# A transformer trunk layer on one core: the first modulation piece cut in two with the context tokens brought in later, more late-modulation chunks ahead of the gates, pooled products two chunks later, and the scores' maximum taken negated

## The chip, the core and the metric

The kernel runs on one core of a Trainium2 chip. The metric is the time of one execution on the device in microseconds (us). The engines are named as in the profile: PE (TensorE: matrix products, with its weight loads as PEld), DVE (VectorE), ACT (ScalarE), POOL (GpSimd) and SP (SyncE, which here issues nearly all DMAs). Each engine works through its own instructions strictly in the order in which they were built.

## What is computed

The layer takes 256 latent tokens `x` and 256 context tokens `ctx`, both of width 2048, in float32. Cut to what matters here:

```
mod   = silu(c)     @ w_mod + b_mod     -> sa, ca, ga, sm, cm, gm   (each 2048 wide)
mod_c = silu(c_ctx) @ w_mod + b_mod     -> sa_c, ca_c, ...
h_c = rmsnorm(ctx) * w * (1 + ca_c) + sa_c ;  h = rmsnorm(x) * w * (1 + ca) + sa
q = rope(rmsnorm(h @ w_q)) ; k = [rope(rmsnorm(h @ w_k)), rmsnorm(h_c @ w_k)] ; v = [h @ w_v, h_c @ w_v]
heads = (softmax(q1 k1 / 8) - lam * softmax(q2 k2 / 8)) @ v          (8 heads, two softmaxes each)
y_a = rmsnorm(heads) @ w_a ;  y_b = (pool(h @ w_p) @ pool_w * pool_scale) @ w_b    (4 groups, windows 2, 4, 8, 16)
x = x + ga * ((sigmoid(h @ w_ga_in) * y_a + sigmoid(h @ w_gb_in) * y_b) @ w_o)
x = x + gm * (relu((rmsnorm(x) * w2 * (1 + cm) + sm) @ w_ff1) ** 2 @ w_ff2)
```

## The kernel before

**Split weights.** Weights arrive in chunks of 128 x 1024 floats (512 KB) in the five buffers `raw`. ACT rounds a chunk to a high part (`whi`, L196) and DVE subtracts to get the rest (`wlo`, L197), three buffers of each; a float32 product is then three fast products: high by high, high by low, low by high (`mm3`, L223). `load_next` (L176) issues one chunk of a written-out order, `stream` (L118 to L163), with its cast and subtraction; `wchunk` (L206) hands chunks out in that order, and loads two ahead.

**First phase (L457 to L506).** The modulation columns `ca` and `sa` are made in eight pieces of 512 numbers (256 channels of each). Piece m takes eight chunks of `w_m` (`mod_chunk`, L319); then ACT copies four rows of the result (`mod_rows`, L327), PE turns them into columns (`mod_columns`, L332), and `hidden` (L348) makes 256 channels of the modulated latent (`hL`) and context (`hC`) tokens. Between the chunks of a piece stand the products of the first half of k and of q (`first_group`, L442) for the channels that are ready: per chunk of `w_k` 24 products (two latent and two context token blocks, 12 each), per chunk of `w_q` 12. Their split chunks lie in a tile of their own, `first`. The four loads of `cT`, the context tokens, stand in the stream right behind piece 0, and their squares and sums (`square_sums`, L431, matmuls at L439) within piece 1. The small table `prq` (rotations, norm weights, lambdas) is loaded at the start by ACT's queue, and DVE makes the rotation tables from it at once (L283 to L303).

**Middle.** `v_group(0)`, then `q_group(1)`, `k_group(1)`, `v_group(1)`, `pooling()` and `gates()` (L799, L800), with the attention's units put between them every 4.4 steps. `k_group` hands over its last step and only then writes out the evacuation of its four PSUM banks (`qk_evac`, L397). `scores` takes the row maxima on DVE (L612), multiplies them by -0.125 (L614), and ACT takes the exponential with scale 0.125 (L617). In `pooling` each group g takes four chunks of `w_p`; the window sums run on POOL, `pool_diff` (L716) on DVE and ACT some ticks later, and `pool_out(g - 1)` (L732, twelve products into `pd`) stands at the end of group g, the last one inside the gates.

**Late modulation.** The other four modulation vectors (`ga`, `cm`, `sm`, `gm`) are made on DVE: per chunk one multiply-add `macc` (L556), 32 chunks for each vector, then a split and two products with a matrix of ones (`late_sum`, L564). `late_gen` (L519) goes one step forward whenever the credit that the rates of the stream add up reaches 1. What is missing of `sm` when the last group of `w_o` is done is made up there, at one go (L819).

**End.** `w_o`, the second norm (`shifted`, `hidden2`), the first MLP block (`ff1_first`), seven more, and `ff2` blocks; the last one multiplies by `gm`, adds, and stores (L933 to L939).

PSUM has 8 banks, used in turn under one tag. Small work tiles share the tag `w2` with nine buffers. A scheduler orders the instructions when the program is built, so their order on an engine is not that of the source.

Of the kernel before, what the change touches and what calls it, by code (L numbers as in the profile page):

```python
# [17 lines left out]
P = 128  # L18
# [30 lines left out]
def layer(ctx: ExitStack, tc, a, out):  # L49
# [65 lines left out]


# [5 lines left out]

    for m in range(9):
        for i in range(8 if m < 8 else 0):
            plan("w_m", m, i)
            if i == 0 and m > 1:
                plan("w_q", 0, m - 2)
            if i == 2 and m > 0:
                plan("w_k", 0, m - 1)
        if m == 0:  # L130
            for i in range(4):
                plan("cT", i)
    for n, ch in (("w_q", 6), ("w_k", 7), ("w_q", 7)):
        plan(n, 0, ch)
    for n, g, rate in (("w_v", 0, 1.0), ("w_q", 1, 1.0), ("w_k", 1, 1.5), ("w_v", 1, 1.5)):
        for ch in range(8):
            plan(n, g, ch, rate=rate)
    for g in range(4):
        for i in range(4):
            plan("w_p", 2 * g + i // 2, i % 2, rate=0.75)  # L140
        if g > 0:
            plan("pool_w", g - 1)
    for g in range(4):
        for n, nk in (("w_gb_in", 8), ("w_b", 4), ("w_ga_in", 8), ("w_a", 4)):
            for ch in range(nk):
                plan(n, g, ch, rate=0.42)
            if g == 0 and n == "w_gb_in":
                plan("pool_w", 3)
# [27 lines left out]
    def load_next():  # L176
        key, rate = stream[len(loaded)]
        src = a[key[0]]
        for i in key[1:]:
            src = src[i]  # L180
        if key[0] in ("cT", "x"):
# [66 lines left out]
    nc.scalar.dma_start(prq, a["prq"])  # L248
# [36 lines left out]
    vec.tensor_copy(wkt, pq("wk"))  # L285
    for i, w in enumerate(("wq", "wk")):
        wv = pq(w)
        for t in range(2):
            vec.tensor_mul(tabs[:, 2 * i, t, :], pq("cos")[:, t * 64:t * 64 + 64], wv)
            so = tabs[:, 2 * i + 1, t, :].rearrange("p (a b f) -> p a b f", a=2, b=2)  # L290
            si = pq("sin")[:, t * 64:t * 64 + 64].rearrange("p (a b f) -> p a b f", a=2, b=2)
            wr = wv.rearrange("p (a b f) -> p a b f", a=2, b=2)
            for b in range(2):
                vec.tensor_mul(so[:, :, b, :], si[:, :, b, :], wr[:, :, 1 - b, :])
    lm = work("lm", [P, 2, 64])
    lam2 = small("lam2", 2)
    for i in range(2):
        vec.tensor_mul(lm[:, i, :], pq(f"lq{i + 1}"), pq(f"lk{i + 1}"))
    vec.reduce_sum(lam2, lm, axis=AX.X)
    act.activation(lam2, lam2, AF.Exp)  # L300
    nlam = pool.tile([P, 1], F32, tag="nlam", name="nlam")
    vec.tensor_sub(nlam, lam2[:, 1:2], lam2[:, 0:1])
    vec.tensor_scalar(nlam, nlam, -LAM0, None, ALU.add)  # L303
    sub8 = pool.tile([P, 1], F32, tag="sub8", name="sub8")
    vec.tensor_scalar(sub8, pr("subln"), 1.0 - LAM0, None, ALU.mult)

# [12 lines left out]
    def mod_chunk(m, i, ps):  # L319
        hi, lo = wchunk("w_m", m, i)  # L320
        for part in (hi, lo):
            for kk in range(2):
                k = 2 * i + kk
                pe.matmul(ps, cv[:, k, :], part[:, kk * 512:kk * 512 + 512], start=(k == 0 and part is hi),  # L324
                          stop=(k == 15 and part is lo))

    def mod_rows(ps):  # L327
        rows = work("rows", [4, 512])
        act.copy(rows, ps[0:4, :])
        return rows  # L330

    def mod_columns(j, rows):  # L332
        pt = bank("modT")
        for i in range(4):
            pe.transpose(pt[:, 4 * i:4 * i + 4], rows[:, i * P:i * P + P], ident[0:4, 0:4])
        ms = small("ms", 16)
        act.copy(ms, pt[:, 0:16])
        m3 = ms.rearrange("p (i c) -> p i c", c=4)
        col = small("col", 8)
        c3 = col.rearrange("p (i c) -> p i c", c=2)  # L340
        vec.tensor_add(c3, m3[:, :, 0:2], m3[:, :, 2:4])
        ks = slice(2 * j, 2 * j + 2)
        vec.tensor_add(c3[:, 0:2, :], c3[:, 0:2, :], b1[:, ks].unsqueeze(2).broadcast_to([P, 2, 2]))
        vec.tensor_mul(c3[:, 0:2, :], c3[:, 0:2, :], pr("nw")[:, ks].unsqueeze(2).broadcast_to([P, 2, 2]))
        vec.tensor_add(c3[:, 2:4, :], c3[:, 2:4, :], pr("bsa")[:, ks].unsqueeze(2).broadcast_to([P, 2, 2]))
        return c3

    def hidden(j, t, c3):  # L348

        src, h = ((xT, hL), (cT, hC))[t]  # L350
        hw = work("hw", [P, 2, T])
        r = rms[t]
        ht = h[j // 4]
        for kk in range(2):
            k8 = (2 * j) % 8 + kk
            u = hw[:, kk, :]
            bias = c3[:, 2 + kk, t:t + 1]
            vec.scalar_tensor_tensor(u, src[:, 2 * j + kk, :], c3[:, kk, t:t + 1], r, ALU.mult, ALU.mult)
# [83 lines left out]
    def first_group(w, bs, j):  # L442

        hi, lo = wchunk(w, 0, j)
        at = tokens(len(bs))
        for t0 in range(0, len(bs), 2):
            for kk in range(2):
                k = 2 * j + kk
                for t in (t0, t0 + 1):
                    xmm([bs[t]], [at[t]], k, hi, lo, slice(kk * 512, kk * 512 + 512), k == 0, k == KT - 1)  # L450
                    yield

    def steps(g, n):
        for _ in range(n):
            next(g)
# [5 lines left out]
    ps = bank("mod")  # L461
    for i in range(8):
        mod_chunk(0, i, ps)
    while len(loaded) < 12:
        load_next()
    sb = bank("ssq")
# [590 lines left out]
```

## Time and profile before

| | us |
|---|---|
| median of 3 runs (1534.69 to 1535.77) | 1535.06 |
| the profiled execution, its own time | 1537.14 |
| its span, first to last instruction | 1535.0 |
| PE busy in it | 1485.2 |
| DVE busy in it | 1063.6 |
| DMA moved in it | 347.82 MB |

The span is what the views cut up; the profiled execution took 2.14 us around its span, and 2.08 us more than the median run. A busy PE is not a PE at full speed: after a pause it runs at a lower granted clock for some microseconds, which the table of stretches shows as PEclk.

### The profile page before, as it was taken

To read this page: it belongs to the slowest core of one execution; us is meant where nothing else is said; L and a number is where in the kernel's file an instruction comes from. 1 tells how busy PE (TensorE), PEld (TensorE's weight loads), DVE (VectorE), ACT (ScalarE), POOL (GpSimd) and SP (SyncE) were. 2 spreads that over 40 slices of the span, in tenths; PEclk is the share of its full clock that TensorE was granted. 3 is DMA by queue.
4 is the path that set the end of the run, shared out by engine and by line. 5 is a ranking of instruction groups with operands and counts; after the bars stand their busy time and mean duration, and the time that the engine had idled before them with its cause. 6 is when DMAs were issued, how large, how long until landed. Compare 5 with 4: busy or idle time off the path is not lost.

```text
span 1535.0 us, 19705 instructions
## 1 busy us (share of the span) xinstructions
PE 1485.2 (97%) x7304; PEld 1238.3 (81%) x7304; DVE 1063.6 (69%) x1291; ACT 756.2 (49%) x1005; POOL 127.0 (8%) x124
## 2 busy tenths in 40 slices
PE   6999999999889999999988999999999999999998
PEld 4777887678778888888867988888888888888887
DVE  6898968777887767666767665666666555555665
ACT  7777534456555444444434554544445454444432
POOL 1000101011230000000000100000000000000170
PEclk8999999999999999999998999999999999999999
DMA  9888576545558878788756677777777666666664
GB/s 344 294 294 311 182 255 224 178 123 165 182 189 278 269 261 263 264 299 269 245 180 205 210 243 248 227 228 233 247 233 243 202 188 192 191 192 192 184 198 139
DMA packets 97439, 347.82 MB, mean 227 GB/s; under 512 B 11072, under 2 KB 11712, under 8 KB 97344
## 3 DMA queue, kind: packets, MB, share of 16 engines
q1 hardware_dynamic: 96624, 345.17, 69.9%
q8 instruction: 57, 0.93, 0.2%
q0 software_dynamic: 576, 1.08, 0.2%
q10 hardware_dynamic: 144, 0.33, 0.1%
q14 instruction: 38, 0.31, 0.1%
HBM read 344.44 MB, written 2.10 MB: 226 GB/s over the span
## 4 chain that ended last, share of the span: by engine, by line
PE 86%; DVE 7%; ACT 3%; DMA 2%; issue 2%; POOL 0%; DVEq 0%; ACTq 0%; POOLq 0%; SPq 0%
PE f L906 13%; PE f L389 8%; PE f L388 8%; PE f L391 8%; PE f L909 7%; PE pg L388 4%; PE pg L389 4%; PE pg L391 4%; DVE wlo L197 2%; PE wo L388 2%; PE pyy L388 2%; PE wo L391 2%; PE pyy L389 2%; PE wo L389 2%; PE pyy L391 2%; PE mod L324 2%
## 5 line engine op out<-in xcount | busy, mean ns | idle before, releaser
L197 DVE TENSOR_TENSOR wlo<-raw,whi 128x1024 fp32r<-128x1024 f32 x501 | 618.1, 1238 | 371.4 <-ACT whi L196 362.7
L196 ACT CAST whi<-raw 128x1024 fp32r<-128x1024 f32 x501 | 523.7, 1048 | 581.8 <-PE f L389 178.1
L906 PE MATMUL f<-h,whi 128*128 128x512 f32 x896 | 224.2, 392 | 0.0
L389 PE MATMUL f<-whi,act 128*128 128x512 f32 x512 | 199.3, 389 | 0.0
L388 PE MATMUL f<-whi,act 128*128 128x512 f32 x512 | 199.3, 389 | 0.0
L906 PEld LDWEIGHTS f<-h,whi 128*128 128x128 f32 x896 | 161.5, 189 | 29.2
L556 DVE SCALAR_TENSOR_TENSOR macc<-raw,sil,macc 128x1024 f32<-128x1024 f32 x122 | 160.1, 1313 | 3.6 <-DMA macc<-in_b_cm_dram 3.5
L391 PE MATMUL f<-wlo,act 128*128 128x512 f32 x512 | 136.8, 389 | 0.0
L909 PEld LDWEIGHTS f<-h,wlo 128*128 128x128 f32 x896 | 122.2, 190 | 8.7
L909 PE MATMUL f<-h,wlo 128*128 128x256 f32 x896 | 124.9, 282 | 0.0
L391 PEld LDWEIGHTS f<-wlo,act 128*128 128x128 f32 x512 | 96.1, 188 | 20.0
L389 PEld LDWEIGHTS f<-whi,act 128*128 128x128 f32 x512 | 96.1, 188 | 19.8
L388 PEld LDWEIGHTS f<-whi,act 128*128 128x128 f32 x512 | 96.1, 188 | 19.8
L388 PE MATMUL pg<-whi,hL 128*128 128x512 f32 x256 | 100.8, 394 | 0.0
L389 PE MATMUL pg<-whi,hL 128*128 128x512 f32 x256 | 100.3, 392 | 0.0
L917 POOL TENSOR_TENSOR rsq<-relu 128x512 f32<-128x512 f32 x28 | 29.2, 1042 | 537.6 <-ACT relu L916 527.4
L391 PE MATMUL pg<-wlo,hL 128*128 128x512 f32 x256 | 68.5, 389 | 0.0
L388 PEld LDWEIGHTS pg<-whi,hL 128*128 128x128 f32 x256 | 48.6, 190 | 10.0
L389 PEld LDWEIGHTS pg<-whi,hL 128*128 128x128 f32 x256 | 48.5, 189 | 10.0
L391 PEld LDWEIGHTS pg<-wlo,hL 128*128 128x128 f32 x256 | 48.0, 188 | 10.1
L388 PE MATMUL wo<-whi,mix 128*128 128x512 f32 x128 | 49.9, 390 | 0.0
L389 PE MATMUL wo<-whi,mix 128*128 128x512 f32 x128 | 49.8, 389 | 0.0
(285 smaller groups left out, 2239.6 us busy)
## 6 DMA issues: line engine op xcount, KB each, us to landing
raw<-in_w_ff_dram SPq DMA_DIRECT2D x240, 512.0 KB, 4.3
raw<-in_w_m_dram SPq DMA_DIRECT2D x64, 512.0 KB, 5.1
raw<-in_w_ga_dram SPq DMA_DIRECT2D x32, 512.0 KB, 4.4
raw<-in_w_cm_dram SPq DMA_DIRECT2D x32, 512.0 KB, 4.6
raw<-in_w_gb_in_dram SPq DMA_DIRECT2D x32, 512.0 KB, 4.5
raw<-in_w_ga_in_dram SPq DMA_DIRECT2D x32, 512.0 KB, 4.5
raw<-in_w_sm_dram SPq DMA_DIRECT2D x32, 512.0 KB, 4.6
raw<-in_w_o_dram SPq DMA_DIRECT2D x32, 512.0 KB, 4.3
```

The lines of the kernel that those rows point to most:

```text
L196: act.copy(hi, raw)
L197: vec.tensor_sub(lo, raw, hi.bitcast(F32))
L324: pe.matmul(ps, cv[:, k, :], part[:, kk * 512:kk * 512 + 512], start=(k == 0 and part is hi), stop=(k == 15 and part is lo))
L388: pe.matmul(banks[t], tok(h, k, 0, tt), wt, start=k == 0, stop=False)
L389: pe.matmul(banks[t], tok(h, k, 1, tt), wt, start=False, stop=False)
L391: pe.matmul(banks[t], tok(h, k, 0, tt), wt, start=False, stop=k == 2 * nk - 1)
L556: pin(vec.scalar_tensor_tensor(acc, raw, sil[:, 0, k:k + 1], acc, ALU.mult, ALU.add))
L906: pe.matmul(ps, hi[:, kk * P:kk * P + P], both(h2, k), start=k == 0, stop=False)
L909: pe.matmul(ps[:, T:2 * T], lo[:, kk * P:kk * P + P], act_slice(h2, k, 0), start=False, stop=k == KT - 1)
L917: gp.tensor_mul(sq, r, r)
```

## The change

- Piece 0 of the modulation is made in two halves of 256 numbers, four chunks each (`w_m0`, products 256 wide), so that the first 128 channels of `hL` are there before the second half is done.
- `cT` is loaded inside pieces 1 and 2, one load behind a chunk; its squares and sums go into piece 2, and the context's channels are made from there on. The context products of a chunk of `w_k` (`kc`) come later than its latent ones (`kx`), from the split chunk that is kept in `first`; a table `carried` says which products stand in which piece. The chunks of `w_q` no longer have a tile of their own but use the three `whi` and `wlo` buffers. The last piece's order is kc 6, kx 7, q 7, kc 7.
- `prq` is loaded by SP in piece 3, and `tables()` (with q's weight already times 0.125) is called in piece 4.
- The rate of the late modulation is 1.5 instead of 1.0 in `v_group(0)` and 1.0 instead of 0.75 in the pooling: 4 chunks more in each.
- `k_group` writes out its evacuation ahead of its last step.
- `pool_out(g - 2)` stands behind the second chunk of group g; the last two stand behind the second and the last chunk of the first gate.
- `reduce_max` negates, the multiplication by -0.125 and the scale of the exponential go.
- The last group of the last `ff2` takes its last two chunks bank by bank (`last=2`).

```diff
+    carried = {1: ((1, "kx", 0), (4, "q", 0)), 2: ((2, "kx", 1), (4, "q", 1)),
+               3: ((0, "kc", 0), (3, "kx", 2), (5, "q", 2), (6, "kc", 1))}
+    for m in range(4, 8):
+        carried[m] = ((0, "kc", m - 2), (2, "kx", m - 1), (4, "q", m - 1))
+    carried[8] = ((0, "kc", 6), (0, "kx", 7), (0, "q", 7), (0, "kc", 7))
...
-    for n, g, rate in (("w_v", 0, 1.0), ("w_q", 1, 1.0), ("w_k", 1, 1.5), ("w_v", 1, 1.5)):
+    for n, g, rate in (("w_v", 0, 1.5), ("w_q", 1, 1.0), ("w_k", 1, 1.5), ("w_v", 1, 1.5)):
...
-            plan("w_p", 2 * g + i // 2, i % 2, rate=0.75)
+            plan("w_p", 2 * g + i // 2, i % 2, rate=1.0)
...
-        if key[:2] in (("w_k", 0), ("w_q", 0)) and key[2] < 7:
+        if key[:2] == ("w_k", 0):
...
-            i = 0 if key[0] == "w_k" else 2
+            i = 2 * (key[2] % 2)
...
+    for half in range(2):
+        ps = bank("mod")
+        for i in range(4):
+            mod_chunk(("w_m0", half), i, ps, 256)
+            if half == 1 and i == 1:
+                cols[0] = mod_columns(0, rows, 1)
+                hidden(0, 0, cols[0], 1)
+        rows = mod_rows(ps, 256)
...
+            if m == 2 and 0 < i < 5:
+                square_sums(cT, gp, sb, i - 1)()
...
+            if m == 4 and i == 1:
+                tables()
+            gens += [first_steps(n, j) for at, n, j in carried[m] if at == i]
+            todo = chain(*gens)
+            steps(todo, 16 if i == 7 else 2 if i < 4 or m == 3 else 1)
...
-        yield from xstat(("w_k", g), bs, tokens(4))
+        for ch, w in enumerate(xstat(("w_k", g), bs, tokens(4))):
+            if ch < 7:
+                yield w
         for t in range(4):
             qk_evac(bs[t], t, g, kT, 2, 3 + t)
+        yield w
...
-            vec.reduce_max(mx[:, p:p + 1], ps, axis=AX.X)
+            vec.reduce_max(mx[:, p:p + 1], ps, axis=AX.X, negate=True)
...
-        vec.tensor_scalar(mx, mx, -0.125, None, ALU.mult)
...
+                    if g > 1 and i == 0 and kc == 1:
+                        pool_out(g - 2)
...
-            if g > 0:
-                pool_out(g - 1)
...
-            for _ in xstat(("w_ff2", b, g), bs, [(at, 0), (at, 1)], nk=4):
+            for _ in xstat(("w_ff2", b, g), bs, [(at, 0), (at, 1)], nk=4, last=2 if b == 7 and g == 3 else 1):
```

How the instructions then stand is shown at three places. The first is PE at the end of piece 0 (`mod` are the modulation products, `modT` the turn into columns, `ssq` the sums of squares of the context, `k` the first k products). Before:

```order
L324 MATMUL mod<-whi,cv 128x512 x2
L324 MATMUL mod<-wlo,cv 128x512 x2
L335 MATMUL modT<-prm,rows 128x4 x4
L324 MATMUL mod<-whi,cv 128x512 x2
L324 MATMUL mod<-wlo,cv 128x512 x2
L439 MATMUL ssq<-sq,mean 128x256 x4
L324 MATMUL mod<-whi,cv 128x512 x2
L324 MATMUL mod<-wlo,cv 128x512 x2
```

And of the change:

```order
L347 MATMUL mod<-whi,cv 128x256 x4
L347 MATMUL mod<-wlo,cv 128x256 x4
L347 MATMUL mod<-whi,cv 128x512 x2
L359 MATMUL modT<-prm,rows 128x4 x2
L347 MATMUL mod<-wlo,cv 128x512 x2
L347 MATMUL mod<-whi,cv 128x512 x2
L347 MATMUL mod<-wlo,cv 128x512 x2
L241 MATMUL w_k_312<-first,hL_94 128x512
```

The context's sums (`ssq`) no longer stand behind the second chunk of piece 1, and the first product of k comes there instead.

The second is DVE between the end of `w_o` and the MLP (`rq_y` is the norm's factor, `yt` the shifted row that PE turns next, `macc` a late chunk, `al` the low part of a finished late vector). Before:

```order
L65 SCALAR_TENSOR_TENSOR rq_y<-rq_t,rq_y 128x2
L65 SCALAR_TENSOR_TENSOR macc<-raw,sil,macc 128x1024
L841 SCALAR_TENSOR_TENSOR yt<-yt,rq_y,sb 128x256
L65 SCALAR_TENSOR_TENSOR macc<-raw,sil,macc 128x1024
L841 SCALAR_TENSOR_TENSOR yt<-yt,rq_y,sb 128x256
...
L65 SCALAR_TENSOR_TENSOR macc<-raw,sil,macc 128x1024 x2
L65 TENSOR_TENSOR al<-macc,ah 128x512 x2
L65 SCALAR_TENSOR_TENSOR yt<-yt,rq_y,sb 128x256 x2
```

And of the change:

```order
L65 SCALAR_TENSOR_TENSOR rq_y<-rq_t,rq_y 128x2
L65 SCALAR_TENSOR_TENSOR yt<-yt,rq_y,sb 128x256 x2
L874 SCALAR_TENSOR_TENSOR yt<-yt,rq_y,sb 128x256 x4
L65 TENSOR_TENSOR h_0_6802<-h2T,h_0_6802 128x512
L65 SCALAR_TENSOR_TENSOR yt<-yt,rq_y,sb 128x256 x2
```

The six late chunks and the split behind them no longer stand between the norm's factor and the rows that PE waits for.

The third is PE at the first pooled product (`pd`; `pin` are the products of `w_p`, `sc`, `aTp` and `ob` belong to the attention). Before, it stands at the start of the third group, behind a unit of the attention:

```order
L611 MATMUL sc<-kT,qT 128x512 x2
L631 MATMUL aTp<-prm,e 128x128 x4
L640 MATMUL ob<-aT,v 128x256 x4
L224 MATMUL pd<-dh,whi 128x256
L224 MATMUL pin<-hL_116,whi 128x256
```

And of the change, two chunks of `w_p` later:

```order
L242 MATMUL pin<-hL_95,whi 128x256
L243 MATMUL pin<-hL_95,wlo 128x256
L241 MATMUL pd<-dh,whi 128x256
L242 MATMUL pd<-dl,whi 128x256
L243 MATMUL pd<-dh,wlo 128x256
```

Forty-eight `pin` products more stand ahead of it than before.

More of the change, by code (lines that the diff above doesn't have):

```diff
@@ L114, in raw_chunk, with chain @@
         return raw
+    def chain(*gens):
+        for g in gens:
+            yield from g
     stream = []
@@ L460, in layer @@
     rms = [rsq(sb[:, 0:T], T, P / D, "aT")]
[L461 to L466, printed above, removed]
[L467 to L469 removed]
+    cols = {}
+    for half in range(2):
+        ps = bank("mod")
+        for i in range(4):
+            mod_chunk(("w_m0", half), i, ps, 256)
[3 more added lines that the diff above has]
+        rows = mod_rows(ps, 256)
```

220 lines of the change are left out of this document (113 added, 107 removed).

## The prediction, made before the changed kernel was run

> **What bounds the kernel now.** I read the page first: shares of the engines, then the chain that ended last.
>
> ```profile
> PE 1485.2 (97%) x7304; PEld 1238.3 (81%) x7304; DVE 1063.6 (69%) x1291; ACT 756.2 (49%) x1005; POOL 127.0 (8%) x124
> PE 86%; DVE 7%; ACT 3%; DMA 2%; issue 2%; POOL 0%; DVEq 0%; ACTq 0%; POOLq 0%; SPq 0%
> ```
>
> PE sets the time. The change leaves its products alone, so it can gain only where PE waits, or runs at a lower granted clock after a wait. The next view is therefore what PE waited for.
>
> ```profile
> PE late L567 <- ACT ah L65: 13.2, 1, 13.2
> PE pd L224 <- ACT dh L220: 9.7, 2, 5.2
> PE ssq L439 <- DVE sq L438: 8.5, 1, 8.5
> PE mod L324 <- ACT whi L196: 4.7, 2, 4.5
> PE v L388 <- ACT e L617: 3.1, 1, 3.1
> ```
>
> Columns: total us, times, longest. These five rows hold 39 us. Last, the table of stretches, cut at these waits (columns: PE, PEld, DVE, ACT, POOL busy with counts, PE clock, DMA share, GB/s).
>
> ```profile
> 14.50:25.10 10.60, 9.49 (x34) 5.49 (x33) 8.18 (x9) 8.45 (x11) 0.63 (x1) 1.00 0.87 320
> 25.10:29.65 4.55, 0.03 (x1) 0.00 (x1) 0.02 (x1) 4.31 (x8) 4.18 (x4) 0.78 1.03 415
> 29.65:37.60 7.95, 7.81 (x20) 5.41 (x21) 7.34 (x13) 5.99 (x8) 0.23 (x1) 0.50 0.93 353
> 48.10:155.00 106.90, 104.25 (x460) 81.92 (x461) 95.98 (x142) 77.72 (x102) 0.00 (x0) 1.00 0.86 300
> 293.10:297.10 4.00, 3.96 (x11) 3.09 (x12) 1.67 (x4) 2.64 (x6) 0.00 (x0) 0.60 0.42 131
> 397.10:402.00 4.90, 4.86 (x23) 4.86 (x23) 2.62 (x5) 2.64 (x8) 1.68 (x5) 0.50 0.48 156
> 437.00:442.00 5.00, 5.00 (x20) 4.35 (x20) 5.00 (x5) 2.98 (x5) 5.00 (x6) 0.63 0.55 179
> 798.40:811.60 13.20, 0.00 (x0) 0.00 (x0) 11.57 (x17) 1.96 (x6) 0.00 (x0) 0.65 0.50 154
> 811.60:819.50 7.90, 7.20 (x26) 5.90 (x27) 7.78 (x15) 4.14 (x6) 1.45 (x2) 0.50 0.41 147
> ```
>
> Every wait from 3 us up has a second price: in the 4 to 8 us behind it the clock is near 0.5, and products take twice their time.
>
> **1. The first phase.** Piece 0 ends at 25.1, and PE then idles 4.55 us.
>
> ```profile
> 20.57 7.91 DMA raw<-in_w_m_dram
> 47.44 0.61 PE L324 MATMUL mod<-wlo,cv 128*128 128x512 f32 x2
> 41.14 1.89 PE L439 MATMUL ssq<-sq,mean 128*128 128x256 f32 x8
> 44.19 0.23 PE k L225
> 165.07 0.39 PE L388 MATMUL v<-whi,hC 128*128 128x512 f32 x1
> ```
>
> The chain there is the load of the next chunk, issued at 20.57 behind four context loads of 512 KB; DMA's share is 1.03, so they were served one after another. The change takes them out of that place. How fast the start then runs is set by DVE: a subtraction of a chunk takes 1.22 us (ACT's cast 1.05).
>
> ```profile
> L197 DVE TENSOR_TENSOR wlo<-raw,whi 128x1024 fp32r<-128x1024 f32 x50 | 59.6, 1219 | 7.5 <-ACT whi L196 7.4
> L196 ACT CAST whi<-raw 128x1024 fp32r<-128x1024 f32 x49 | 51.0, 1050 | 17.1 <-DMA raw<-in_w_m_dram 9.6 <-PE mod L324 2.0 <-DVE wlo L197 1.7
> 11.89 2.51 DVE L197 TENSOR_TENSOR wlo<-raw,whi 128x1024 fp32r<-128x1024 f32 x2 [0.32 <-ACT whi L196]
> prq<-in_prq_dram ACTq DMA_DIRECT2D x1, 320.0 KB, 3.5
> ```
>
> DVE's first subtraction starts at 11.9 before; without the 320 KB of `prq` ahead of it (1 us at the 320 GB/s of the rows), at 10.9. To the end of piece 1 stand 19 subtractions (16 modulation chunks, one of k, one of q, and the next piece's first), 23.2 us, and the norm factor, two columns, two latent channel blocks and the waits for casts and turned rows, which I put at 7.4 together (before, DVE gave 10.6 - 8.2 = 2.4 us of the stretch 14.5 to 25.1 to such waits alone). That is 41.5 us, with k's and q's first 24 products done. Before, the same point without q's products is 48.1, but the context's sums are done there. What is left then: before 468 products of 512 columns, which took from 48.1 to 165.07 less 1.36 us of six v products within, 115.6 us or 0.247 each; after 456 of them, 112.6, and the context's sums, 3.8 us at the full clock (half of them, eight rows of L439, took 1.89). I add 2.5 us, an estimate: the twenty-odd small instructions of `tables()`, hidden at the start before, now stand where DVE is 95.98 of 106.9 us busy (20 times the 0.16 us of the shortest row of DVE below is 3.2), and ACT gets the context's eight squares in the piece with most casts. End: 41.5 + 112.6 + 3.8 + 2.5 = 160.4 against 163.7: **3.3 us less**. The ends: with products at the 0.23 us of the row above and no added stall 12 us less; with every chunk behind q's held up 0.3 us, since q's split chunk now takes one of the three `whi` buffers (7 pieces of 3 such chunks, 6.3 us), 3 us more. SP and POOL: SP only gets four loads later and `prq` in piece 3; POOL's four adds move with the squares.
>
> **2. The evacuation of k.** PE waits 3.0 us for a bank that ACT frees only after two exponentials, and then runs 4.0 us at 0.60: 3.0 + 4.0 x 0.4 = 4.6 us. In the changed order ACT's copies of k stand ahead of those exponentials, so two banks come free earlier. The four copies each wait for DVE's part of the one before, so the third bank is late by about 0.9: **3.7 less**, between 0 and 5. [...]
>
> **3. The pooled products.** Two waits of 5.2 and 4.5, and cold stretches of 4.9 us at 0.50 and 5.0 at 0.5 behind them: 9.7 + 2.5 + 2.5 = 14.7 us. Both have another 48 products (5.8 us by the `pin` rows below, the first and the last of 48) and a unit of attention, 2 us or more, ahead of them after the change, and only the last 5 us were missing, so both should go. What is late next is DVE.
>
> ```profile
> 356.20:442.00 85.80, 76.12 (x517) 68.45 (x516) 66.24 (x100) 48.79 (x89) 21.46 (x36) 0.92 0.57 180
> 419.92 1.65 DVE L556 SCALAR_TENSOR_TENSOR macc<-raw,sil,macc 128x1024 f32<-128x1024 f32 x1
> 356.20 0.28 PE L224 MATMUL pin<-hL,whi 128*128 128x256 f32 x1
> ...
> 361.84 0.28 PE L226 MATMUL pin<-hL,wlo 128*128 128x256 f32 x1
> 410.22 0.16 DVE L614 TENSOR_SCALAR mx<-mx 128x2 f32<-128x2 f32 x1
> ```
>
> The stage lasts 85.8 us, and without the waits 71.1. DVE has 66.2 us of work in it, gets four multiply-adds more (1.28 us each, 1.65 beside POOL's sums), and loses six scalings of 0.16: 70.7. An engine in order that feeds PE is not 99% busy; the long stretch with a nearly unbroken PE, 48.1 to 155, has it at 90%. By 93% the stage lasts 76, and 4.9 of the 14.7 are given back: **9.8 less**, between 14.7 and 5. The tiles `dh` and `dl` live longer, in the nine buffers that POOL's sums and the exponentials use too; that is within these ends.
>
> **4. The turn to the MLP.** Before, DVE does six late chunks and a split after the norm's factor.
>
> ```profile
> 801.88 0.16 DVE L65 SCALAR_TENSOR_TENSOR rq_y<-rq_t,rq_y 128x2 f32<-128x2 f32 x1
> 801.96 1.28 DVE L65 SCALAR_TENSOR_TENSOR macc<-raw,sil,macc 128x1024 f32<-128x1024 f32 x1
> 812.82 0.88 DVE L65 SCALAR_TENSOR_TENSOR yt<-yt,rq_y,sb 128x256 f32<-128x256 f32 x2
> 815.53 1.23 PE L224 MATMUL f<-h,whi 128*128 128x256 f32 x4 [0.68 <-ACT h L65]
> ```
>
> After, the two `yt` come at 802.1 instead of 812.82, and the first product at 804.8 instead of 815.53: 10.7 us. PE's four products for `sm`'s sums move into `w_o`, 0.9 us. Still left is a pause from 798.4 to 803.1, so the cold stretch behind it stays. **9.8 less**, between 8 and 10.7. The eight chunks come from here and the MLP; four go to `v_group(0)`, where DVE has room:
>
> ```profile
> 160.00:215.00 55.00, 55.00 (x256) 45.46 (x255) 43.46 (x72) 25.85 (x45) 7.90 (x4) 1.00 0.55 165
> ```
>
> 43.5 and 5.1 of 55 us is 88%: nothing, at worst 2 us.
>
> **5. The end.**
>
> ```profile
> 1529.24 0.76 DVE L937 TENSOR_TENSOR o<-f,gm_bc 128x256 f32<-128x256 f32 x2 [6.12 <-PE f L391]
> 1530.58 0.75 DVE L937 TENSOR_TENSOR o<-f,gm_bc 128x256 f32<-128x256 f32 x2
> ```
>
> Two banks are evacuated behind the last product, 1.34 us each; after, the first is done 2.7 us before PE ends: **1.4 less**, between 1 and 2.7. The negated maximum has no row. The nearest is the plain one:
>
> ```profile
> L612 DVE TENSOR_REDUCE mx<-sc x12: 674/682/691, 355.5 to 409.3; 128x1 f32<-128x512 f32 x12
> ```
>
> I take the same 0.68 us. Were it twice that, DVE would have 12 times 0.68, 8 us more in the pooling, all of which would reach PE; were it free, the pooling would give back nothing of its 4.9.
>
> **Sum.** 3.3 + 3.7 + 9.8 + 9.8 + 1.4 = 28.0 us off the profiled execution, 1537.1 to 1509.1; the median run lies 2.1 lower, so 1535.1 - 28.0 = **1507.1**.
>
> **The rivals.** *All waits go and nothing comes in their place*: 8 + 4.6 + 14.7 + 9.8 + 1.4 = 38.5 less, 1496.6. For it: DMA and ACT are nowhere full; against it: DVE at 90% in the first phase. *DVE takes the freed places*: the first phase gains nothing, the pooling 5: 0 + 3.7 + 5 + 9.8 + 1.4 = 19.9, 1515.2. *The pooled products wait as long as before*, because POOL's sums wait for buffers that `dh` and `dl` hold, and so move back with them: the wait list of POOL shows such waits.
>
> ```profile
> POOL za L702 <- DVE d L726: 14.7, 1, 14.7
> POOL za L702 <- PE pd L225: 1.9, 2, 1.5
> ```
>
> Then term 3 is nil: 1516.9. Most of that 14.7 is an idle POOL, so I give it little.
>
> *A cold start.* The changed start has many short pauses. If the clock fell to 0.5 from 14.5 to 41.5, PE's 20.4 us of products there would take 40.8 in a stretch of 27: 13.8 more, 1520.9. Against it: in 14.5 to 25.1 the clock stays 1.00 with pauses at nearly each low part. [...]
>
> *Slower.* q's split chunk sits in the shared buffers over chunks 5, 6 and 7 of a piece, so two are left and cast and subtraction of the next chunk can't run ahead: 1.05 + 1.22 = 2.27 us uncovered, on 21 chunks 47.7 us, 1535.1 - 28.0 + 47.7 = 1554.8. It decides from 1.3 us per chunk. Against it: between two modulation chunks PE has 0.9 us of products of its own and some of q and k, which cover most.
>
> **How the numbers follow.** Forecast 0.52, all waits gone 0.16, DVE takes the places 0.14, pooled products still wait 0.06, cold start 0.07, slower 0.05. The range takes in all but the last, from a little under the second to the cold start: 1494 to 1521. Some 0.2% (3 us) is what a measurement can tell from no change; only the slower case with a smaller hold-up could land there, so faster 0.95, same 0.01, slower 0.04.
>
> **What would show it.** Right: no PE wait at `pd`, none at `v` for the exponential, the wait at the MLP cut to about 5 us, and v's first products near 161; DVE over 90% busy in the pooling. Wrong: a clock under 1 between 15 and 60 us (cold start); pieces longer than 18 us (buffers); `pd` waiting for `dh` again; or PE waiting for `wlo` in the pooling by more than 5 us.

## The result, and the profile after

The changed kernel takes **1520.61 us**, median of 4 runs (1518.57 to 1522.38), against 1535.41 of the kernel before (1534.69 to 1536.12, 4 runs beside them): 14.8 us less, a ratio of 0.9903 with a 95% interval of 0.9886 to 0.9920. The forecast was 1507.1, 28.0 less, in a range of 1494 to 1521: the sign is right and the time lies in the range, 0.4 us from its upper end; of the gain about half came.

The profiled execution of after took 1519.78 us (span 1517.7), 17.4 less than the 1537.14 of the one before; that one lay 1.7 above the median of the four runs and this one 0.8 below. The page's first line of after, and then what PE waits for in it (total us, times, longest):

```profile
PE 1480.7 (98%) x7336; PEld 1232.8 (81%) x7336; DVE 1063.2 (70%) x1280; ACT 755.7 (50%) x1007; POOL 129.3 (9%) x124
PE ssq L461 <- DVE sq L460: 7.7, 1, 7.7
PE h2T L881 <- DVE yt L65: 4.2, 1, 4.2
PE mod L347 <- DVE wlo L214: 3.9, 8, 0.7
PE mod L347 <- ACT whi L213: 3.0, 5, 1.6
PE qkT L447 <- POOL qm L440: 3.0, 2, 2.0
PE pg L413 <- DVE wlo L214: 2.5, 1, 2.5
PE aTp L665 <- ACT e L651: 2.4, 1, 2.4
PE pd L243 <- DVE wlo L214: 1.4, 1, 1.4
```

The four waits that the forecast wanted gone are gone or cut: 13.2 at the MLP is 4.2, and the two for `dh`, the one for an exponential and the 4.5 us behind the context's loads are not there. But there are new ones: many short ones at `mod`, two for `qm`, three for a split or an exponential in the pooling.

To see where the time went, I cut both executions at the same work. Most of these rows give all products of a tile; behind the comma stand the first and the last start: the second query group, the pooling, and `y_b`'s products, of before and then of after. The others are single products, with their start in front. (The pooling of before starts at 356.20, by the row in the prediction.)

```profile
L388 PE MATMUL q<-whi,hL x32: 389/389/389, 210.2 to 230.6; 128*128 128x512 f32 x32
L388 PE MATMUL pyy<-whi,yb x64: 389/389/402, 466.2 to 675.3; 128*128 128x512 f32 x64
797.32 1.07 PE L391 MATMUL wo<-wlo,mix 128*128 128x512 f32 x4
```

```profile
162.60 0.39 PE L411 MATMUL v<-whi,hL 128*128 128x512 f32 x1
170.99 0.39 PE L410 MATMUL v<-whi,hC 128*128 128x512 f32 x1
L410 PE MATMUL q<-whi,hL x32: 389/389/389, 217.2 to 237.6; 128*128 128x512 f32 x32
L241 PE MATMUL pin<-hL,whi x128: 278/283/680, 357.8 to 429.6; 128*128 128x256 f32 x128
L410 PE MATMUL pyy<-whi,yb x64: 389/389/402, 460.1 to 670.1; 128*128 128x512 f32 x64
792.15 1.07 PE L413 MATMUL wo<-wlo,mix 128*128 128x512 f32 x4
799.23 1.22 PE L241 MATMUL f<-h,whi 128*128 128x256 f32 x4 [0.68 <-ACT h L65]
```

Sixteen v products stand ahead of 162.83 in after (159.20 to 162.60), 3.63 us that belong behind the first phase, and six in before (1.36 us). So the phase ends at 170.99 - 3.63 = 167.4, against 163.7 before.

| stage | before | after | difference | forecast |
|---|---|---|---|---|
| start to the end of the first phase | 163.7 | 167.4 | +3.7 | -3.3 |
| to the second query group | 46.5 | 49.8 | +3.3 | 0 |
| to the pooling | 146.0 | 140.6 | -5.4 | -3.7 |
| pooling, to `y_b`'s first product | 110.0 | 102.3 | -7.7 | -9.8 |
| to the last group of `w_o`'s last chunk | 331.1 | 332.0 | +0.9 | +0.9 |
| turn, to the MLP's first product | 18.2 | 7.1 | -11.1 | -10.7 |
| to the end | 719.5 | 718.5 | -1.0 | -1.4 |
| sum | | | -17.3 | -28.0 |

Four stages came out within 2 us of the forecast. The first two are on the wrong side, by 7.0 and 3.3 us, and the pooling is 2.1 short.

**The first phase.** The table of stretches, before and then after (us of PE, PEld, DVE, ACT, POOL with counts, granted clock, DMA share, GB/s; the last row is the part of after ahead of its low clock):

```profile
26.00:44.00 18.00, 14.21 (x47) 10.77 (x48) 11.61 (x16) 13.46 (x19) 3.63 (x3) 0.72 0.94 333
44.00:56.00 12.00, 11.20 (x50) 8.37 (x49) 11.22 (x18) 8.02 (x12) 0.00 (x0) 1.00 0.88 282
```

```profile
26.00:44.00 18.00, 15.07 (x58) 9.63 (x56) 12.62 (x16) 10.12 (x13) 0.00 (x0) 1.00 0.93 344
44.00:56.00 12.00, 9.85 (x25) 6.02 (x25) 9.84 (x13) 10.31 (x18) 4.93 (x3) 0.57 0.77 276
36.70:45.20 8.50, 5.73 (x21) 3.26 (x20) 3.16 (x3) 3.62 (x4) 0.00 (x0) 1.00 1.00 400
```

From 26 to 44 us after makes 58 products where before made 47: the forecast's gain is there. From 44 to 56 it makes 25, at a clock of 0.57, and before made 50, at 1.00. Both have PE nearly full behind that (104.25 of 106.9 us from 48.1 to 155.0 before, 101.45 of 104.0 from 56 to 160 in after), so these 12 us decide the phase. Around the turn from piece 1 to piece 2, on PE and on ACT of after (start, us, and in brackets the idle time and what ended it):

```profile
42.88 0.73 PE L347 MATMUL mod<-wlo,cv 128*128 128x512 f32 x2 [0.53 <-DVE wlo L214]
45.23 1.08 PE L347 MATMUL mod<-whi,cv 128*128 128x512 f32 x2 [1.61 <-ACT whi L213]
```

```profile
37.95 1.05 ACT L213 CAST whi<-raw 128x1024 fp32r<-128x1024 f32 x1 [1.80 <-DMA raw<-in_w_m_dram]
40.52 1.05 ACT L213 CAST whi<-raw 128x1024 fp32r<-128x1024 f32 x1 [1.53 <-PE w_q L242]
43.65 0.57 ACT L352 COPY rows<-mod 4x512 f32<-4x512 f32 x1 [2.08 <-PE mod L347]
44.13 1.04 ACT L213 CAST whi<-raw 128x1024 fp32r<-128x1024 f32 x1
46.86 0.17 ACT L361 COPY ms<-modT 128x16 f32<-128x16 f32 x1 [1.69 <-PE modT L359]
```

ACT waits for a load (DMA's share is 1.00 from 36.7 to 45.2, the context's four loads among them), then for a `w_q` product that holds a buffer, then for the piece's last product, since `rows` stands ahead of the next chunk's cast. PE has no other work: the latent products of piece 1 are used up, and the context's are not there yet. Before, those stood at this turn, 1.2 us behind the start of piece 1's last products (47.44):

```profile
48.66 0.50 PE L224 MATMUL k<-first,hC 128*128 128x512 f32 x1 [0.61 <-ACT hC L359]
```

### The profile page after: what moved, and what is told of

It is laid out like the page before. It is cut to its first block, busy times and chain, and to the rows that moved or that the text cites. A ratio compares the mean times of both kernels' runs of the same rounds, so it can differ in the third digit from the quotient of the medians.

```text
span 1517.7 us, 19767 instructions
## 1 busy us (share of the span) xinstructions
PE 1480.7 (98%) x7336; PEld 1232.8 (81%) x7336; DVE 1063.2 (70%) x1280; ACT 755.7 (50%) x1007; POOL 129.3 (9%) x124
## 4 chain that ended last, share of the span: by engine, by line
PE 88%; issue 3%; DVE 3%; DMA 3%; ACT 1%; POOL 1%; DVEq 0%; SPq 0%; ACTq 0%; POOLq 0%
PE f L939 14%; PE f L411 8%; PE f L410 8%; PE f L413 8%; PE f L942 7%; PE pg L413 4%; PE pg L410 4%; PE pg L411 4%; PE pyy L410 2%; PE wo L410 2%; PE wo L413 2%; PE wo L411 2%; PE pyy L413 2%; PE pyy L411 2%; PE v L411 2%
## 5 line engine op out<-in xcount | busy, mean ns | idle before, releaser
L214 DVE TENSOR_TENSOR wlo<-raw,whi 128x1024 fp32r<-128x1024 f32 x507 | 628.6, 1244 | 365.2 <-ACT whi L213 350.9
L213 ACT CAST whi<-raw 128x1024 fp32r<-128x1024 f32 x507 | 529.8, 1047 | 587.3 <-PE f L411 178.1
L588 DVE SCALAR_TENSOR_TENSOR macc<-raw,sil,macc 128x1024 f32<-128x1024 f32 x128 | 166.2, 1299 | 1.4 <-DMA raw<-in_w_cm_dram 0.8
L410 PEld LDWEIGHTS pg<-whi,hL 128*128 128x128 f32 x256 | 48.1, 188 | 10.1 <-issue 0.2
L411 PEld LDWEIGHTS pg<-whi,hL 128*128 128x128 f32 x256 | 48.1, 188 | 10.1 <-issue 0.2
L411 PE MATMUL wo<-whi,mix 128*128 128x512 f32 x128 | 49.8, 389 | 0.0
```

The lines of the kernel that those rows point to most:

```text
L213: act.copy(hi, raw)
L214: vec.tensor_sub(lo, raw, hi.bitcast(F32))
L410: pe.matmul(banks[t], tok(h, k, 0, tt), wt, start=k == 0, stop=False)
L411: pe.matmul(banks[t], tok(h, k, 1, tt), wt, start=False, stop=False)
L588: pin(vec.scalar_tensor_tensor(acc, raw, sil[:, 0, k:k + 1], acc, ALU.mult, ALU.add))
```

## The experiments

Each run is given by its median and its ratio to before in the same session; stages are those of the table, from one profiled execution each.

**old_first.** The change without its first phase: the code of before up to the evacuation of the first k and q, with the other edits of the diff.

> Every part of the change but the first phase, which is that of before. By the trace after, the new first phase hands over at 167.36 us against 163.71, so it costs 3.7 us: without it 1520.6 - 3.7 = 1516.9. By the forecast's own term it saves 3.3: without it 1523.9. If the new first phase is also what makes the rotated q late in the value products behind it (the waits of 2.0 and 0.9 us for POOL's qm), these go too: 1513.9.

1514.72 us, ratio 0.9860 (0.9847 to 0.9872): faster than after, and the intervals lie apart. There is no wait for `qm`, and from the context's first v product (164.3) to the second query group (209.4) it takes 45.1 us, as before (165.1 to 210.2), though the rate is 1.5. So the new first phase costs time by itself, and its meeting with the rate costs some more. (Its pooling, the same code as in after, takes 104.8 us and not 102.3; the wait of 2.4 us for an exponential is 3.2 here.)

**first_only.** The other way round: the new first phase, with the rates, `k_group`, `pool_out`, the maximum and the end of before.

> The new first phase alone, the rest as before. By the trace after it costs 3.7 us: 1535.4 + 3.7 = 1539.1. By the forecast's term it saves 3.3: 1532.1. If the waits for qm belong to the first phase and not to the rate of the late modulation, 1542.1.

1540.91 us, ratio 1.0032 (1.0021 to 1.0043): slower than before. From 44 to 56 us it makes 29 products at a clock of 0.57; the waits for `qm` are 0.6 us in all. The forecast's sign for this part falls. Its way from the context's first v product to the second query group is 43.8 us, with the rate of 1.0.

**v0_to_q.**

```diff
-    for n, g, rate in (("w_v", 0, 1.5), ("w_q", 1, 1.0), ("w_k", 1, 1.5), ("w_v", 1, 1.5)):
+    for n, g, rate in (("w_v", 0, 1.0), ("w_q", 1, 1.5), ("w_k", 1, 1.5), ("w_v", 1, 1.5)):
```

> After, with the rate of the late modulation back at 1.0 in the first value group and at 1.5 instead of 1.0 in the second query group, so the same four chunks stand one group later. If the four chunks there make DVE late for q's evacuation, both waits for qm go and the time is 1520.6 - 3.0 = 1517.6, up to 0.5 lower. If the waits come from the longer first phase, they stay: 1520.6. If DVE is then late in the second query group, the waits only move: 1520.6 with a new wait between 217 and 240 us.

1533.21 us, ratio 0.9973 (0.9961 to 0.9984): 12 us above after, which none of the three expected cases had. The waits for `qm` do shrink, to 0.5. But two new ones come, on PE, each with products at half speed behind it (a clock of 0.50 from 352.2 to 356 and from 406.2 to 414), and the pooling takes 112.0 us instead of 102.3.

```profile
352.23 2.08 PE L646 MATMUL sc<-kT,qT 64*128 64x512 f32 x4 [4.89 <-ACT kT L448]
406.21 0.79 PE L599 MATMUL late<-ah,ones 128*128 128x512 f32 x1 [4.22 <-ACT ah L237]
```

Four multiply-adds of 1.3 us moved by one group cost 12 us, far more than their own 5.1: what was late was the last k for the scores, and the split of the late modulation in the middle of the pooling.

**cover.** q's first chunk behind piece 1's last.

```diff
-    carried = {1: ((1, "kx", 0), (4, "q", 0)), 2: ((2, "kx", 1), (4, "q", 1)),
+    carried = {1: ((1, "kx", 0), (7, "q", 0)), 2: ((2, "kx", 1), (4, "q", 1)),
```

> After, with q's first chunk loaded behind the last chunk of piece 1 instead of its fifth, so that its 12 products (2.7 us) stand between piece 1 and piece 2. If the stretch from 44 to 54 us runs at half clock because nothing covers the turn of the piece, its granted clock rises to 1.00 and the time falls by about 4.3 us (8.8 us at half clock) to 1516.3. If DVE's pace sets the start anyway and the low clock only fills its waits, nothing moves: 1520.6.

1519.40 us, ratio 0.9890 (0.9877 to 0.9903), not to be told from after; the first v product of the context comes at 170.4 instead of 170.99. From 44 to 56 us the clock is 0.85, but it is low earlier, where q's products were taken away:

```profile
36.30:40.70 4.40, 2.71 (x8) 1.37 (x9) 2.96 (x3) 2.09 (x2) 0.00 (x0) 1.00 1.03 419
40.70:43.80 3.10, 3.10 (x9) 2.19 (x9) 1.79 (x2) 1.62 (x2) 0.00 (x0) 0.51 1.02 404
```

Covering the turn moves the low clock and gains 0.6 us at most, not 4.3: the four kernels that have after's first phase as it is (after, first_only, v0_to_q, p_to_gates) reach that product at 169.7 to 171.0, so 0.6 can't be told from nothing. PE's work was short in the whole stretch, not at one place: in cover it is busy for 2.71 of the 4.40 us from 36.3 and for 4.31 of the 6.70 from 45.0.

**shift_only.** Before, with only the lines of the diff on `pool_out` and `pool_w`.

> Before with one edit: the pooled products stand two chunks later. If both waits at pd (5.2 and 4.5 us) and the low clock behind them (5.0) go and nothing comes in their place, 14.7 less: 1535.4 - 14.7 = 1520.7. If the work on DVE sets the pace of the pooling by itself, without the four added multiply-adds, a part comes back as waits for split chunks, as after (6.3 us of waits there): 1535.4 - 8.4 = 1527.0. If the products then wait as long in their new place: 1535.4.

1531.66 us, ratio 0.9976 (0.9964 to 0.9988). The pooling takes 104.1 us (463.6 less 359.5) instead of 110.0, so 5.9 of 14.7 come, although no multiply-add was added: in place of the two waits stand 1.2, 0.7 and 0.7 at `pd` and 3.3 for POOL. The time falls by less, 3.7, and lies wider than that of the others (1527.54 to 1537.55, 12 runs). From the second k group to the pooling the profiled execution took 126.5 us and before 124.3. Both have the wait of 3.1 us for an exponential there; in before 4.0 us at a clock of 0.60 follow it (293.1 to 297.1), here 6.0 us at 0.51, which makes 1.3 of the 2.2:

```profile
295.10:301.10 6.00, 5.98 (x14) 4.74 (x15) 1.67 (x4) 2.62 (x6) 0.00 (x0) 0.51 0.31 87
```

**rates_only.** Before, with 1.5 for `w_v` 0 and 1.0 for `w_p`.

> Before with one edit: eight chunks of the late modulation earlier, by the rates of the first value group and the pooling. The turn to the MLP loses its six multiply-adds, 11.3 us by the trace after, and the last group of w_o gains 1.0 for the late products: 1535.4 - 10.3 = 1525.1, if DVE's added work in the pooling lies beside the two waits at pd, which are still there. If it reaches PE there, 4 multiply-adds of 1.3 us are given back: 1530.3.

1528.91 us, ratio 0.9958 (0.9945 to 0.9970), between the two. The turn loses its multiply-adds (the wait there is 4.2), and the pooling lasts 110.3 against 110.0: the added work does lie beside the waits at `pd`, which grow from 9.7 to 12.0 in three. Of the 11.1 us won at the turn 2.2 are lost between `y_b`'s first product and the end of `w_o`, where 1.0 were expected. The parts don't add up: shift_only's 3.7 and the 6.5 here, with the k group's 5.4 and the end's 1.0, make 16.6, and old_first, which has all four, gains 21.5.

**sq_late.** After, with the context's loads, squares and sums later in piece 2, and so the context's first channels and k's first context products later in piece 3; the cut shows the loads and the sums. (In this kernel a part of k's first context products reads weights that a later chunk has replaced. Their number is the same, but its output is wrong, so its time is only a hint.)

```diff
-            if m == 1 and i > 5 or m == 2 and i < 2:
-                plan("cT", (8 * m + i - 14))
+            if m == 2 and 1 < i < 6:
+                plan("cT", i - 2)
...
-            if m == 2 and 0 < i < 5:
-                square_sums(cT, gp, sb, i - 1)()
+            if m == 2 and i > 3:
+                square_sums(cT, gp, sb, i - 4)()
```

> After, with the four context loads behind the chunks 2 to 5 of piece 2 instead of the chunks 6 and 7 of piece 1 and 0 and 1 of piece 2, and their squares and sums as much later. Between 44 and 56 us the start fell from 13 products ahead of before to 12 behind it. If it is the squares on ACT (8 of 0.63 us) and POOL's adds beside DVE's subtractions that hold up the casts and splits there, at least half of these 25 products come back, 3 us or more: 1517.6 or less. If it is only the chain of the turn of the piece (rows, transposes, columns, hidden), they lie beside it: 1520.6.

1518.43 us, ratio 0.9892 (0.9874 to 0.9910). The context's first v product comes at 168.1 instead of 170.99, 2.9 earlier, as the first theory had it; the time itself can't be told from after's. The run sq_late2 below does it with the right weights.

**k_first.** k's last context products ahead of q's.

```diff
-    carried[8] = ((0, "kc", 6), (0, "kx", 7), (0, "q", 7), (0, "kc", 7))
+    carried[8] = ((0, "kc", 6), (0, "kx", 7), (0, "kc", 7), (0, "q", 7))
```

> After, with k's last 12 context products ahead of q's last 12 instead of behind them, so that k's four banks are complete 2.7 us earlier. The waits for POOL's qm (2.0 and 0.9 us) stand only where the new first phase and the rate of 1.5 meet. If they come from k's late end, which leaves DVE the evacuation and the extra chunks at one time, they shrink to 0.3 or less: 1517.9. If the four extra chunks alone decide, they stay: 1520.6.

1521.30 us, ratio 0.9907 (0.9893 to 0.9922): no change, and the waits for `qm` are 3.3 us in three. The order of the last products is not the cause.

**p_to_gates.** Four multiply-adds from the pooling to the gates.

```diff
-            plan("w_p", 2 * g + i // 2, i % 2, rate=1.0)
+            plan("w_p", 2 * g + i // 2, i % 2, rate=0.75)
...
-                plan(n, g, ch, rate=0.42)
+                plan(n, g, ch, rate=0.46)
```

> After, with the rate of the late modulation back at 0.75 in the pooling and 0.46 instead of 0.42 in the gates, so four multiply-adds (5.1 us of DVE) leave the pooling for the gates. If DVE's load sets the pace of the pooling, the three waits there (2.4 for an exponential, 1.4 and 2.5 for a split) shrink by 4 to 5 us: 1516.1. If the waits come from the order alone (a split queued behind the wrong instruction on DVE), they stay or move: 1520.6 within 1.5. If the gates have no room for four more, up to 5.1 are given back there: 1520.6 as well, but with the pooling shorter and a wait behind 460 us.

1520.55 us, ratio 0.9896 (0.9880 to 0.9913): the same as after, and the pooling lasts 102.5 against 102.3. What PE waits for between 400 and 460 us has other names:

```profile
PE pd L241 <- ACT dh L237: 2.2, 1, 2.2
PE osum L685 <- POOL osq L681: 1.6, 1, 1.6
PE pin L243 <- DVE wlo L214: 1.1, 1, 1.1
```

This is less of a test than it looks, for the work did not leave the stage: DVE is busy for 84.7 us in it, and for 86.6 in after. Cut at the last `pin` product, after and then p_to_gates:

```profile
357.80:429.60 71.80, 67.95 (x496) 60.81 (x495) 62.34 (x87) 43.70 (x78) 18.09 (x30) 1.00 0.63 196
429.60:460.10 30.50, 28.02 (x136) 23.11 (x136) 24.27 (x36) 15.61 (x25) 9.16 (x13) 1.00 0.69 222
356.80:425.30 68.50, 67.41 (x495) 60.43 (x494) 56.17 (x80) 42.62 (x77) 17.77 (x27) 1.00 0.60 190
425.30:459.30 34.00, 30.21 (x138) 24.69 (x137) 28.57 (x42) 17.61 (x27) 10.05 (x17) 0.95 0.66 203
```

The part with `w_p` has 6.2 us less of DVE's work and is 3.3 us shorter; the part behind it has 4.3 more and is 3.5 longer. So the run does not show that DVE's load is without effect. That the order has one shows in the largest wait of after, on DVE and PE:

```profile
441.00 0.58 DVE L758 TENSOR_TENSOR za<-za,prm 128x7 f32<-128x7 f32 x1 [2.53 <-POOL za L744]
444.45 0.17 DVE L758 TENSOR_TENSOR za<-za,prm 128x7 f32<-128x7 f32 x1 [2.87 <-POOL za L744]
444.56 1.23 DVE L214 TENSOR_TENSOR wlo<-raw,whi 128x1024 fp32r<-128x1024 f32 x1
```

```profile
445.84 1.20 PE L413 MATMUL pg<-wlo,hL 128*128 128x512 f32 x4 [2.48 <-DVE wlo L214]
```

DVE stands idle for 5.4 us on POOL's window sums, with the split that PE needs queued behind. DVE's load does not explain this wait; the place of the window sums in its queue does.

**sq_late2.** As sq_late, with the context's first channels made at the start of piece 3, ahead of the products that read them:

```diff
+                    if m == 3:
+                        rms.append(rsq(sb[:, 0:T], T, P / D, "aT"))
+                        hidden(0, 1, cols[0], 1)
+                        hidden(1, 1, cols[1], 1)
                     cols[2 * m - 2] = mod_columns(2 * m - 2, rows)
```

> After, with the context's loads behind the chunks 2 to 5 of piece 2 and its squares and sums as much later, the context's first channels made at the start of piece 3. If the squares and POOL's adds hold up the casts and splits at the turn from piece 1 to piece 2, the value products of the context start near 168 us instead of 170.99 and the time is 1517.6. If the work only moves to a place that is as full, both stay: 1520.6.

1516.73 us, ratio 0.9871 (0.9850 to 0.9891), 3.9 us below after by the medians; the intervals overlap by a hair (0.9886 to 0.9891). The context's first v product comes at 168.3, outside the 169.7 to 171.0 of after's first phase. Its stretches, and ACT at the turn:

```profile
26.00:44.00 18.00, 15.85 (x64) 10.86 (x64) 13.68 (x18) 12.19 (x16) 0.00 (x0) 1.00 0.89 302
44.00:56.00 12.00, 9.47 (x36) 5.93 (x35) 10.57 (x15) 10.45 (x16) 5.01 (x3) 1.00 1.03 413
```

```profile
40.25 1.05 ACT L213 CAST whi<-raw 128x1024 fp32r<-128x1024 f32 x1 [0.95 <-DMA raw<-in_w_m_dram]
42.15 0.58 ACT L352 COPY rows<-mod 4x512 f32<-4x512 f32 x1 [0.84 <-PE mod L347]
43.58 0.16 ACT L361 COPY ms<-modT 128x16 f32<-128x16 f32 x1
```

The next chunk's cast now stands ahead of `rows`, at 40.25, and the columns come at 43.58 instead of 46.86; 100 products instead of 83 are made from 26 to 56 us, and the clock stays at 1.00. Loads and squares were moved together, and which of the two does it was not tried apart; after's squares begin only at 46.93, behind the late turn, so the loads have the better case.

**ctx_inside.** old_first, with the same idea on the first phase of before:

```diff
-        if m == 0:
-            for i in range(4):
-                plan("cT", i)
+            if m == 1 and i < 4:
+                plan("cT", i)
```

and the squares and sums behind the chunks 1 to 4 of piece 1.

> old_first with one edit: the four context loads stand behind the chunks 0 to 3 of piece 1 instead of ahead of them, as the squares and sums do. The wait of 4.5 us for the chunk behind the loads and the low clock behind it (4.0 us) go: up to 8.5 less than old_first, 1506.2. If instead the squares on ACT and POOL's adds hold up the casts and splits of piece 1 there, as they do in after at the turn to piece 2, most of it is given back: 1514.7, or above.

1518.92 us, ratio 0.9878 (0.9858 to 0.9898), not faster than old_first (two of its five runs lie at 1514.6 and 1515.0, three at 1518.9 to 1520.0, the profiled one among the three). In that one the context's first v product comes at 167.1, 2.8 later, and the pooling takes 106.9 us, 2.1 more. The wait of 4.5 us for the loads is gone, and PE waits 3.5 us for `hC` at 48.95, with a clock of 0.72 from 44 to 56. Taking the loads away from one place here only moved the wait to where the context is needed.

**late_sq_v0.** sq_late2, with `w_v` 0 back at 1.0 and the gates at 0.46.

> sq_late2 with the rate of the late modulation back at 1.0 in the first value group and 0.46 instead of 0.42 in the gates, which took four chunks without a wait in p_to_gates. If the four chunks in the value group cost the two waits for POOL's qm (2.0 and 0.9 us), the second query group starts 2.5 us or more earlier against the context's first value products than in sq_late2 (46.2 us between the two there), and the time is 1516.7 - 3.0 = 1513.7. The late modulation's split then falls behind another chunk of the pooling; if the order there decides more than the load, the pooling (102.3 us from its first product to the first product of y_b) changes by up to 10 us, as it did in v0_to_q, and takes the gain: 1516 to 1524.

**1514.28 us**, ratio 0.9855 (0.9838 to 0.9871): faster than before and after. From the context's first v product (168.1) to the second query group (211.9) it takes 43.8 us instead of 46.2, the waits for `qm` are 0.5 in all, and the pooling lasts 101.5. So the four chunks in the value group were what cost it; first_only and v0_to_q, with the rate of 1.0 there, have the same 43.8. old_first, at 0.9860, is as good.

## Why the prediction was right, and where its steps failed

**That the time lies in the range is in part luck.** The upper end, 0.4 us away, came from the cold start, whose account did not come true (below); and of the terms, the first had the wrong sign and the pooling a reason that did not hold.

**The first phase failed, in sign.** The step was "to the end of piece 1 stand 19 subtractions ... That is 41.5 us", and behind it 112.6 us of products and 3.8 of sums with 2.5 us of added stall. The last product of piece 1 starts at 42.88 and ends at 43.6, 2.1 later; that is the small miss. From there to 167.4 it takes 123.8 us instead of 118.9, because I let PE run at full pace from the first turn on. At the turn of a piece, `rows` to columns to channels, PE needs other products; before these were the context's, and the change had moved them to piece 3. I had priced what the change removed and not what stood at the turn. I had also written that DMA is nowhere full, against my own row with 1.03; in after the moved loads fill it again, 1.00 from 36.7 to 45.2, and the cast at 37.95 waits 1.80 us for its chunk.

old_first and first_only show the sign. The 3.7 us are one pair of executions: the four kernels with the old first phase (before, old_first, shift_only, rates_only) come to the context's first v product at 164.3 to 166.2, the four with the new one at 169.7 to 171.0, and by the means, less the v products ahead, the new one costs 2.9. Some 2 of these hang on where the context's loads and squares stand (168.1 to 168.3 in sq_late, sq_late2 and late_sq_v0). Even there the phase ends some 4 us later than forecast, with the clock at 1.00 from 26 to 56 in sq_late2. That the missing products of the context make this rest is not shown: no run puts them back behind the new piece 0, and cover, with q's products in their place, gained nothing that can be told.

**The rates in `v_group(0)` failed in size:** "nothing, at worst 2 us", and the stage took 3.3 more. I had priced them by DVE's busy share, 43.5 and 5.1 of 55 us. But the share does not tell. The same 39 us of before, old_first and after:

```profile
160.00:199.00 39.00, 39.00 (x184) 32.19 (x183) 34.45 (x64) 20.04 (x36) 7.90 (x4) 1.00 0.53 155
160.00:199.00 39.00, 39.00 (x185) 32.22 (x185) 36.55 (x67) 19.78 (x36) 7.69 (x4) 1.00 0.55 174
160.00:199.00 39.00, 37.13 (x172) 30.35 (x170) 34.87 (x68) 19.17 (x36) 6.40 (x3) 1.00 0.59 194
```

DVE works 34.5, 36.6 and 34.9 us, and PE waits only in the last. There DVE comes late to the steps that make `qm`, with multiply-adds among them (1.28 us each, at 186.14, 187.45 and 192.58), POOL's sum over `qm` begins at 196.84, and PE waits for it at 199.17. The rate of 1.5 costs nothing under the old first phase (45.1 us to the second query group in before and in old_first) and 2.4 under the new one (46.2 in after and sq_late2, 43.8 in the three runs at 1.0). The other 0.9 comes with the new first phase alone.

**The evacuation of k gained more:** 5.4 instead of 3.7, past its upper end of 5. From the second k group's first product to the pooling it takes 118.6 to 119.1 us in after, old_first, cover, sq_late, k_first, p_to_gates, sq_late2, ctx_inside and late_sq_v0, and 124.3 to 126.5 in the four kernels without it (v0_to_q, with its wait of 4.9, is the exception). I had kept 0.9 us for a third bank that comes late; that lateness does not show. The 0.8 beyond the whole price of 4.6 stay open; in shift_only the low clock behind this wait lasted 6.0 us, longer than the 4.0 us that I took.

**The pooling came near by a reason that did not hold.** 7.7 against 9.8, and waits of 6.3 us in place of the old ones, where I had 4.9 given back. But I gave them back because DVE would be 93% busy, and it was 85% (86.6 of 102.3 us; 87% up to the last `pin` product). shift_only has waits of 6.1 us there without one added multiply-add, and the same pooling lasts 101.5 to 106.9 us in other runs, with other instructions late. What stands at the head of DVE's queue makes the largest wait of after, 2.5 us; how much its load makes beside that is open, since p_to_gates only moved the work within the stage. That the sum came out 2.1 off is luck as much as sense. (The row that I showed for the second cold stretch has 0.63, since it is cut late; from the wait's end, 435.45 to 440.45, the clock is 0.50, so the 2.5 us stand.)

**The turn to the MLP and the end were right:** 11.1 less 0.9 against 9.8, and 1.0 against 1.4. The four late products do stand in `w_o`, and DVE goes from the factor to `yt`. At the end, the first bank is done beside the last products:

```profile
1512.18 1.07 PE L413 MATMUL f<-wlo,act 128*128 128x512 f32 x4
1513.29 0.76 DVE L970 TENSOR_TENSOR o<-f,gm_bc 128x256 f32<-128x256 f32 x2 [1.30 <-PE f L413]
```

The negated maximum costs what the plain one did (682 ns then, 683 now), as taken:

```profile
L647 DVE TENSOR_REDUCE mx<-sc x32: 671/683/693, 259.5 to 406.0; 128x1 f32<-128x512 f32 x32
```

**The rivals.** The time, 1520.6, is that of "a cold start", 1520.9, but not by its account: the clock is low for 9.3 us, not 27, which costs some 4.6 us of products (9.3 x 0.49, an estimate) and not 13.8, and the rest of the miss is elsewhere. Against that rival I had set the row of 14.5 to 25.1, where PE was 90% busy; the stretch that mattered came later and was emptier (67% from 36.7 to 45.2). In cover a low clock did come behind short pauses alone: 8 products in 4.4 us, no pause over 0.58 us, and 0.51 behind them. The slower rival's mechanism, q's chunk in the shared buffers, is seen at three casts, which wait 3.6 us in all for `w_q` products (1.53 of it at 40.52), not at 21 chunks. Of the signs that I had named, the end of the first phase near 161 and DVE over 90% busy in the pooling did not come; of the signs of being wrong two did, a clock under 1 between 15 and 60 us and pieces longer than 18 us: from one turn (`modT`) to the next pieces 1 and 2 took 20.0 and 26.4 us, the five behind them 16.5 to 17.5.

The sum missed by 10.7 us: 7.0 in the first phase, 3.3 in the value group and 2.1 in the pooling, less 1.7 that the k group gave more; the other terms cancel. Between the medians of the four runs each, 2.6 us less show than between the profiled executions, which is the scatter of either. (The lower end that I gave for the first phase, 12 us, is 13.5 by its own numbers; the sum doesn't use it.)

## What to carry to other kernels

When work is moved, ask what it was covering, and what it will meet, not only what it was waiting for: the first phase lost its wait of 4.5 us for the loads and came out longer, and some 2 us of that go with the place at the next turn that the same loads got. Room on an engine in order was here a matter of what stood at its head, and its busy share told little: old_first's value group took four multiply-adds more on a DVE that worked 36.6 of 39 us, and after's did not with 34.9. And a stage's room must be read with the neighbour that it will have, since the rate of 1.5 cost nothing behind the old first phase and 2.4 us behind the new one.

## What the hardware showed that was not expected

The granted clock fell without a wait of 3 us ahead of it, where the forecast had only counted it behind such waits. In cover the longest pause on PE from 36.3 to 40.7 us is 0.58 us, with 8 products in 4.4 us, and the clock behind it is 0.51; in after the longest is 1.61, and the clock is 0.51 from 45.2 to 54.5:

```profile
45.20:54.50 9.30, 8.35 (x20) 4.77 (x21) 8.34 (x12) 7.64 (x13) 3.43 (x3) 0.51 0.73 276
```

In sq_late2, with 36 products from 44 to 56 and a longest pause of 1.05, it stays at 1.00. So the longest pause does not tell these three apart: behind 0.58 and 1.61 us the clock was low, and behind 1.05 it was not. What goes with the low clock in them is how little PE does over some microseconds: it was 62% busy ahead of it in cover (over 4.4 us) and 67% in after (8.5 us), and 79% in sq_late2 (12 us). Three stretches, cut by hand, don't show that this is the cause. Nor was the price of one wait fixed: behind the same 3.1 us the low clock lasted 4.0 us in before (0.60) and 6.0 in shift_only (0.51).
